# A hybrid encoder block on one core: weight sums moved between the pairs of an MLP, a value projection taken into the input stage, and an operand loaded one step earlier

## The chip, the cores and the metric

The kernel runs on one core of one Trainium2 chip. The metric is the device time of one execution in microseconds, as the median of several runs. The engines are named as in the profile: PE is TensorE's matrix multiplication and PEld its weight load, DVE is VectorE, ACT is ScalarE, POOL is GpSimd, and SP is SyncE, whose queue issues all the transfers here.

## The reference, cut to what matters

The block has 1024 tokens of width 1024. One projection of the normed input feeds two mixers: a bidirectional gated delta rule with 8 heads (mixer A), and a dilated window attention with 3 groups of 4 heads (mixer B). Then comes an MLP of width 4096.

```python
h = rmsnorm(x, ln_mix_pre)
proj = h @ w_in                      # q, k, v, z, 32 decay/beta columns (AF), mixer B's q, k, v, gates
o_a = rmsnorm(delta_rule(q, k, v, decay, beta)) * silu(z)     # both directions summed
o_b = windows combined over three groups                      # values: columns C_VB
y = (gate_a * (o_a @ w_branch_a) + gate_b * (o_b @ w_branch_b)) @ w_out
x = x + rmsnorm(y, ln_mix_post)
f = relu(rmsnorm(x, ln_mlp_pre) @ w_ff1) ** 2
x = x + rmsnorm(f @ w_ff2, ln_mlp_post)
```

All inputs and outputs are 32-bit floats.

## The kernel before

**Products.** Each operand of a large product is split into a rounded part and a remainder (`split`, L86 on ACT and L87 on DVE), and each product is three matrix instructions (`mm3`, L110 to L112): hi by hi, hi by lo, lo by hi. A projection (`proj`) loads 128 columns of weights, splits them, and takes 8 blocks of the inner dimension by 3 instructions for each half of 512 tokens, 48 instructions in all, into a PSUM bank.

**Order.** Tiles come from pools with a fixed number of buffers. When the kernel is built, a planner lays the instructions of each engine into one order, by the order of the program and by its own estimate of when operands are ready; each engine then runs its list in that order, and so does SP's queue of transfers. An instruction that waits holds back what stands behind it on its engine.

**Input stage.** `input_norm` loads 8 tiles of x, norms them, transposes them (L216) and writes the operand hT in two halves (b = 0, 1). After each half it runs the AF projection (128 columns, of which 32 are used; the result `ab` is transposed, columns on partitions) and one half of branch gate 0. `gates` transposes `ab` back (L253) and works out the decays. Twelve further gate projections stand at low priority as work for PE to fall back on (`gm`). Then `key_phase` runs for 8 heads; after every second one an attention head starts. `att_values` computes mixer B's values for two heads at a time: for each of 8 blocks of tokens, 8 by 3 instructions with hT as the weights and 256 columns of w_in moving.

**Delta stage.** For each head `delta_proj` (q, v, z), `delta_prep`, `delta_chain` (8 dependent steps) and `delta_tail`; the chain of head h runs beside the projections of head h+1. For the last head z's projection stands behind `delta_prep`. hT's memory is then given up, `oa` and `ob` tiles take its place, and `merge_b` loads and splits `ob` (four tiles) ahead of its first product; the last chain runs beside `merge_b`.

**MLP.** Both products use a scheme of seven block products for a two by two split. The sums of blocks that it needs are made on DVE. For w_ff1's product, "pair" c (`ff1_pair`, 3 to 15) loads two 512 KB tiles of w_ff1, forms s1 to s4 (L1137 to L1140, tiles `mid`), and runs seven products of 12 instructions (L1151) in the order a11, s3, s2, a22, s1, a12, s4; `keep` copies a bank on ACT before the next product adds onto it. `f_blocks` then forms the sums of the results and stores seven blocks (`d_f`). `w_blocks` makes w_ff2's sums for the second product, 16 blocks of 1 MB: load `wq`, four subtractions (L983 to L986), four stores (`d_T`). It is stepped once behind each pair, twice behind pairs 3, 4 and 5. `wq` shares one buffer (tag `t1`). `ff2` then runs the seven products over 8 pieces each, from `d_f`, w_ff2 and `d_T`; in the last product the last two pieces run bank by bank (6 times 8 and then 4 banks), so that each bank's `block` (L1043, L1045) and `finish` (L1052) can start.

Of the kernel before, what the change touches and what calls it, by code (L numbers as in the profile page):

```python
# [70 lines left out]
class Kern:  # L71
# [109 lines left out]
    def input_norm(self):  # L181
# [4 lines left out]
        self.ab = self.abp.tile([128, S], F, name="ab")  # L186
        with ExitStack() as es:
# [55 lines left out]
    def gates(self):  # L243

        nc, a, cp = self.nc, self.a, self.cp
        with ExitStack() as es:
            p = self.pool("gates", ctx=es)
            ab = self.ab
# [255 lines left out]
    def att_values(self, g, j, p):  # L504
# [6 lines left out]
        W = [self.wtile(wv[:, 4 * b:4 * b + 4, col:col + 256], [128, 4, 256]) for b in range(2)]  # L511
        V = p.tile([128, 8, 256], F, name="V", tag="V", bufs=1)
        d = self.d_v[g, j // 2]
        for b in range(4):
# [144 lines left out]
    def delta_proj(self, h, p, z_later=False):  # L659
# [12 lines left out]
        W = self.wsplit(self.wload(w_in, C_ZA + 128 * h, 8))  # L672
        z_proj = lambda: self.proj(w_in, C_ZA + 128 * h, self.hT, 8, (0, 1), z_evac, W=W)
        if not z_later:
            z_proj()
        return qT, vT, zs, z_proj
# [160 lines left out]
    def merge_b(self, p, tp, between):  # L837

        nc, a = self.nc, self.a
        PT = lambda shape, tag, bufs, dt=F: p.tile(shape, dt, name=tag, tag=tag, bufs=bufs)  # L840
        H, L = PT([128, 4, S], "ob_hi", 1, R), PT([128, 4, S], "ob_lo", 1, R)
        for k in range(4):
            cut = lambda x: [x[:, k, 0:512], x[:, k, 512:1024]]
            self.load_split(self.d_ob[k].rearrange("p (n i) -> p n i", n=2), cut(H), cut(L))
        for d in range(8):
# [6 lines left out]
            self.proj(a["w_branch_b"], 128 * d, (H, L), 4, (0, 1), evac)  # L852
# [120 lines left out]
    def w_blocks(self, p, pt):  # L973

        nc, V = self.nc, self.nc.vector
        for k in range(16):
            w = pt.tile([128, 4, 512], F, name="wq", tag="t1", bufs=1)
# [9 lines left out]
            for n, x in (("t3", t3), ("t1", b12), ("t2", b22), ("t4", b21)):  # L987
# [3 lines left out]
    def ff2(self, p, pe, tmp):  # L991
# [9 lines left out]
        def product(bank, fn, w, first, last=False):  # L1001
            def pieces(j):
                fr = p.tile([128, 2, 512], F, name="f_raw", tag="mid", bufs=3)
# [3 lines left out]
                for k in range(2):  # L1007
                    x = [p.tile([128, 512], R, name=f"f_{n}", tag=f"x_{n}", bufs=5) for n in ("hi", "lo")]
# [9 lines left out]
            n = 6 if last else 8  # L1018
            for j in range(n):
# [3 lines left out]
            if last:  # L1023
                rest = pieces(6) + pieces(7)
                for t in range(4):
                    for i, x in enumerate(rest):
                        mul(t, *x, False, i == 3)
# [64 lines left out]
    def mid_blocks(self, h, pt, p):  # L1092
# [6 lines left out]
        t1 = pt.tile([128, 4, 512], F, name="t1", tag="t1", bufs=1)  # L1099
        new = lambda: p.tile([128, 2, 512], F, name="mid", tag="mid", bufs=3)  # L1100
# [27 lines left out]
    def ff1_pair(self, c, rhs, pf, p, tmp):  # L1128
# [5 lines left out]
        sA, sB = (p.tile([128, 2, 4, 128], F, name="mid", tag="mid", bufs=3) for _ in range(2))  # L1134
# [9 lines left out]
        def product(i, bank, src, r, first):  # L1144
            pool, tag, bufs = (self.wp, "w", 2) if i in (0, 3) else (p, "x", 5)
            X = [pool.tile([128, 4, 128], R, name=f"{tag}_{n}", tag=f"{tag}_{n}", bufs=bufs) for n in ("hi", "lo")]
            self.split(*X, src)
            for k in range(4):
                for n, (x, y) in enumerate(((0, 0), (0, 1), (1, 0))):
                    start = first and k == 0 and n == 0  # L1150
                    nc.tensor.matmul(bank, X[x][:, k], r[y][:, k], start=start, stop=k == 3 and n == 2,  # L1151
                                     skip_group_check=not first)

# [5 lines left out]
        f0, f1 = (pf.tile([128, S], F, name="f", tag="f", bufs=2) for _ in range(2))  # L1159
# [4 lines left out]
        p7 = keep(B)  # L1164
        product(2, A, s2, rhs["t2"], False)
# [13 lines left out]
        self.f_blocks(c, f0[:, lo], f1[:, lo], f0[:, hi], f1[:, hi], pf)  # L1179

    def mlp(self, h, early, pf, tmp):
# [3 lines left out]
        with ExitStack() as es:  # L1185
# [21 lines left out]
            sums = self.w_blocks(p, pt)  # L1207
# [18 lines left out]
def build(tc, a, dbg=None):  # L1226
    with ExitStack() as ctx:
# [51 lines left out]
        with ExitStack() as es:  # L1279
            p = k.pool("delta", ctx=es)  # L1280
            qT, vT, zs, _ = k.delta_proj(0, p)
            state = k.delta_prep(0, p, qT, vT)
            for h in range(NH):
                out = k.delta_chain(h, p, **state)
                z = zs
                if h < NH - 1:
                    qT, vT, zs, z_proj = k.delta_proj(h + 1, p, h == NH - 2)
                    state = k.delta_prep(h + 1, p, qT, vT)
                    if h == NH - 2:
                        z_proj()  # L1290
# [3 lines left out]
                        pb = k.pool("ob", ctx=es_b, side="right")  # L1294
# [63 lines left out]
```

## Time and profile before

| | |
|---|---|
| median of 3 runs | 2233.14 us (2232.93 to 2233.23) |
| profiled execution | 2226.74 us, span 2225.0 us |
| PE, PEld | 2154.0 us (97%), 1818.4 us (82%) |
| DVE, ACT, POOL | 1504.5 us (68%), 869.3 us (39%), 61.2 us (3%) |
| matrix instructions | 11571 |
| DMA | 381.65 MB, mean 172 GB/s |
| granted clock | 0.991 of full speed |

The span is the time from the first to the last instruction of the profiled execution; its own time is 1.7 us more, and the median of the runs lies 6.4 us above that. Durations below come from the profiled execution. PE's busy time counts each instruction from its start to a modelled end, and ends overlap the next start, so an instruction's cost in a stream is read from the distance between starts.

### The profile page before, as it was taken

What the parts mean: (1) busy time and instruction counts of PE and PEld (TensorE: products, weight loads), DVE (VectorE), ACT (ScalarE), POOL (GpSimd) and SP (SyncE); (2) the same over time, 40 slices, a digit from 0 to 9 for tenths busy, and PEclk for the clock granted to TensorE, in tenths of its full rate; (3) what the DMA queues carried; (4) which work ended last, traced back from release to release, by engine and by line L of the source; (5) the groups of instructions that cost most, each with busy time, mean ns of one, the idle gap of its engine ahead of it and who ended that gap; (6) DMA issues with size and microseconds to landing.
All of it is one profiled execution on the core that took longest, in us unless ns stands there. A gap on an engine that the chain in (4) does not pass through costs nothing.

```text
span 2225.0 us, 31006 instructions
## 1 busy us (share of the span) xinstructions
PE 2154.0 (97%) x11571; PEld 1818.4 (82%) x11571; DVE 1504.5 (68%) x2656; ACT 869.3 (39%) x1820; POOL 61.2 (3%) x90
## 2 busy tenths in 40 slices
PE   7999999999999999999999999999988999999998
PEld 6877888889778878888888877989866777888877
DVE  5647563999599546777777764475966767544565
ACT  5333343322412333333333332344544555444443
POOL 0211211000000000000000000000000000000000
PEclk9999999999999999999999999999998999999999
DMA  5554746343722657434344338573667877866674
GB/s 179 175 170 129 232 128 192 125 136 100 186 81 76 168 171 196 131 104 115 114 114 119 100 114 282 168 237 105 193 213 260 275 264 260 280 193 191 194 253 139
DMA packets 339486, 381.65 MB, mean 172 GB/s; under 512 B 85540, under 2 KB 243196, under 8 KB 338312
## 3 DMA queue, kind: packets, MB, share of 16 engines
q1 hardware_dynamic: 339336, 379.67, 55.2%
q8 instruction: 91, 1.49, 0.3%
q14 instruction: 59, 0.48, 0.1%
HBM read 264.03 MB, written 118.73 MB: 172 GB/s over the span
## 4 chain that ended last, share of the span: by engine, by line
PE 77%; DVE 9%; DMA 8%; ACT 4%; issue 2%; SPq 1%; DVEq 0%; ACTq 0%
PE mm L112 13%; PE mm L110 13%; PE mm L111 13%; PE acc L1016 5%; PE mm L1016 4%; PE tr L1016 4%; PE acc L1151 3%; PE tr L808 2%; PE gm L110 2%; PE gm L112 2%; PE gm L111 2%; DMA w_raw<-in_w_ff 2%; PE ao L586 2%; DMA wq<-in_w_ff 2%; PE acc L110 1%
## 5 line engine op out<-in xcount | busy, mean ns | idle before, releaser
L110 PE MATMUL mm<-hT_hi,w_hi 128*128 128x512 f32 x960 | 391.1, 407 | 1.4 <-ACT xpad L336 1.0
L111 PE MATMUL mm<-hT_lo,w_hi 128*128 128x512 f32 x960 | 388.5, 405 | 0.0
L112 PE MATMUL mm<-hT_hi,w_lo 128*128 128x512 f32 x960 | 387.5, 404 | 0.7 <-DVE w_lo L87 0.7
L87 DVE TENSOR_TENSOR w_lo<-w_raw,w_hi 128x1024 fp32r<-128x1024 f32 (+1 forms) x219 | 253.6, 1158 | 148.3 <-ACT w_hi L86 146.4
L86 ACT CAST w_hi<-w_raw 128x1024 fp32r<-128x1024 f32 (+1 forms) x219 | 215.1, 983 | 322.5 <-PE mm L111 191.7
L110 PEld LDWEIGHTS mm<-hT_hi,w_hi 128*128 128x128 f32 x960 | 181.5, 189 | 34.6 <-ACT xpad L336 1.5
L112 PEld LDWEIGHTS mm<-hT_hi,w_lo 128*128 128x128 f32 x960 | 181.3, 189 | 34.0 <-DVE w_lo L87 2.8
L111 PEld LDWEIGHTS mm<-hT_lo,w_hi 128*128 128x128 f32 x960 | 181.6, 189 | 31.3 <-issue 0.9
L87 DVE TENSOR_TENSOR f_lo<-f_raw,f_hi 128x512 fp32r<-128x512 f32 x112 | 77.0, 692 | 115.8 <-ACT f_hi L86 115.7
L341 DVE SCALAR_TENSOR_TENSOR cu<-xpad,conv,cu 128x1024 f32<-128x1024 f32 x96 | 125.3, 1306 | 3.3
L86 ACT CAST f_hi<-f_raw 128x512 fp32r<-128x512 f32 x112 | 69.5, 621 | 148.3 <-PE tr L1016 79.4
L432 DVE TENSOR_TENSOR XA<-XB 128x62 f32<-128x62 f32 (+30 forms) x124 | 106.2, 857 | 20.2 <-ACT XB L428 17.7
L110 PE MATMUL mm<-w_hi,hT_hi 128*128 128x256 f32 x384 | 108.0, 282 | 0.3 <-ACT V L522 0.3
L435 DVE TENSOR_TENSOR XB<-XB,XA 128x62 f32<-128x62 f32 (+30 forms) x124 | 106.2, 857 | 3.0
L112 PE MATMUL mm<-w_hi,hT_lo 128*128 128x256 f32 x384 | 107.9, 281 | 0.0
L111 PE MATMUL mm<-w_lo,hT_hi 128*128 128x256 f32 x384 | 107.9, 281 | 0.0
L577 ACT ACTIVATE P<-lg,st 128x256 f32<-128x256 f32 (+1 forms) x96 | 45.4, 473 | 111.2 <-DVE st L574 109.3
L110 PE MATMUL gm<-hT_hi,w_hi 128*128 128x512 f32 x208 | 83.4, 401 | 0.7 <-ACT bg L653 0.5
L112 PE MATMUL gm<-hT_hi,w_lo 128*128 128x512 f32 x208 | 81.9, 394 | 0.0
L111 PE MATMUL gm<-hT_lo,w_hi 128*128 128x512 f32 x208 | 81.7, 393 | 0.0
L1016 PE MATMUL acc<-w_hi,f_hi 128*128 128x512 f32 x192 | 75.3, 395 | 3.1 <-ACT w_hi L86 3.1
L1016 PE MATMUL acc<-w_lo,f_hi 128*128 128x512 f32 x192 | 75.2, 392 | 0.0
(357 smaller groups left out, 5016.3 us busy)
## 6 DMA issues: line engine op xcount, KB each, us to landing
w_raw<-in_w_in SPq DMA_DIRECT2D x85, 512.0 KB
w_raw<-in_w_ff SPq DMA_DIRECT2D x62, 512.0 KB
wq<-in_w_ff SPq DMA_DIRECT2D x32, 512.0 KB
f_raw<-d_f_s SPq DMA_DIRECT2D x32, 512.0 KB
w_raw<-d_t SPq DMA_DIRECT2D x32, 512.0 KB
d_f_s<-s SPq DMA_DIRECT2D x48, 256.0 KB
d_t<-wq SPq DMA_DIRECT2D x48, 256.0 KB
f_raw<-d_f_a SPq DMA_DIRECT2D x24, 512.0 KB
```

The source lines that it names most:

```text
L86: self.nc.scalar.copy(H, src)
L87: self.nc.vector.tensor_tensor(L, src, H, op=OP.subtract)
L110: t.matmul(p, lH, rH, start=first, stop=False)
L111: t.matmul(p, lH, rL, start=False, stop=False)
L112: t.matmul(p, lL, rH, start=False, stop=last)
L341: nc.vector.scalar_tensor_tensor(u, xp[:, t:t + S], cw[:, t:t + 1], u, op0=OP.mult, op1=OP.add)
L432: nc.vector.tensor_tensor(tv, XB[:, 0:j, j:j + 1].to_broadcast([128, j, n]), XB[:, j:j + 1, j + 1:64].to_broadcast([128, j, n]), op=OP.mult)
L435: nc.vector.tensor_tensor(dst, dst, tv, op=OP.add)
L577: nc.scalar.activation(P[:, 0:W], lg[:, 0:W], AF.Exp, bias=nm, scale=-1.0, accum_out=Z)
L586: nc.tensor.matmul(o[:, oc:oc + 128], V[:, kt], PT[:, 128 * n:128 * n + 128], start=n == 0, stop=n == len(keys) - 1)
L1016: nc.tensor.matmul(bank[t], x, y, start=start and first and n == 0, stop=stop and n == 2, skip_group_check=not first)
L1151: nc.tensor.matmul(bank, X[x][:, k], r[y][:, k], start=start, stop=k == 3 and n == 2, skip_group_check=not first)
```

## The change

It has three parts. First, the input stage: the AF projection and its transposes go. Instead, 288 columns (the 256 value columns of mixer B's first two heads and the 32 AF columns) are loaded and split once, and for each of the 8 token blocks 24 instructions with hT as weights and 288 columns moving give the values, which go to memory, and the AF results, with tokens on partitions, which stay in `tok`. `att_values` for those two heads only loads them. Second, the delta stage: z's projection of the last head stands with its q and v, and `load_ob` runs before the last `delta_prep` and no longer inside `merge_b`. Third, the MLP: `w_blocks` is cut in two steps (load; sums and stores) that are called between the products of a pair, with two buffers; t3 is formed in place from t2; `f_blocks` of a pair is called after the second product of the next one. In exchange `mid` has 2 buffers where it had 3, and the split operands `x` 4 where they had 5; the last product's bank-by-bank part covers one piece where it covered two.

```diff
@@ input_norm
-                    W = self.wload(a["w_in"], C_AF, 8)
+                    wv = a["w_in"].rearrange("(k p) c -> p k c", p=128)
+                    W = p.tile([128, 8, 288], F, name="wv_raw")
+                    nc.sync.dma_start(W[:, :, 0:256], wv[:, :, C_VB:C_VB + 256])
+                    nc.sync.dma_start(W[:, :, 256:288], wv[:, :, C_AF:C_AF + 32])
...
-                if b == 0:
-                    W = self.wsplit(W)
...
-                self.proj(a["w_in"], C_AF, self.hT, 8, (b,),
-                          lambda hf, q: nc.scalar.copy(self.ab[:, 512 * hf:512 * hf + 512], q), W=W)
                 if b == 0:
                     Wg = self.wsplit(Wg, self.gp, 1)
+                    w2 = [p.tile([128, 8, 288], R, name=f"wv_{n}") for n in ("hi", "lo")]
+                    for n in range(2):
+                        self.split(*(x[:, 4 * n:4 * n + 4] for x in (*w2, W)))
                 self.branch_gate(0, W=Wg, halves=(b,))
+                for t in range(4 * b, 4 * b + 4):
+                    q = self.pp.tile([128, 288], F, name="mm", tag="mm", bufs=self.mm_bufs)
+                    tok = slice(128 * t, 128 * t + 128)
+                    for k in range(8):
+                        self.mm3(q, [x[:, k, tok] for x in self.hT], [x[:, k] for x in w2], k == 0, k == 7)
+                    v = p.tile([128, 256], F, name="v0", tag="v0", bufs=2)
+                    nc.scalar.copy(v, q[:, 0:256])
+                    nc.vector.tensor_copy(self.tok[:, t], q[:, 256:288])
+                    nc.sync.dma_start(self.d_v[0, 0][tok], v)
@@ gates
-            tok = p.tile([128, 8, 32], F, name="tok")
-            for b in range(2):
-                q = self.pp.tile([128, 512], F, name="tr", tag="sm", bufs=4)
-                for t in range(4):
-                    nc.tensor.transpose(q[:, 128 * t:128 * t + 128],
-                                        ab[:, 512 * b + 128 * t:512 * b + 128 * t + 128], self.ident)
-                nc.vector.tensor_copy(tok[:, 4 * b:4 * b + 4, :],
-                                      q.rearrange("p (t c) -> p t c", t=4)[:, :, 0:32])
+            tok = self.tok
@@ att_values
+        if g == 0 and j == 0:
+            nc.sync.dma_start(V, d.rearrange("(n p) c -> p n c", p=128))
+            return V
@@ build
-                    qT, vT, zs, z_proj = k.delta_proj(h + 1, p, h == NH - 2)
-                    state = k.delta_prep(h + 1, p, qT, vT)
+                    qT, vT, zs = k.delta_proj(h + 1, p)
                     if h == NH - 2:
-                        z_proj()
                         k.ctx_h.close()
...
+                        ob = k.load_ob(pb)
+                    state = k.delta_prep(h + 1, p, qT, vT)
@@ w_blocks
-            w = pt.tile([128, 4, 512], F, name="wq", tag="t1", bufs=1)
+            w = pt.tile([128, 4, 512], F, name="wq", tag="t1", bufs=2)
...
-            t3 = p.tile([128, 2, 512], F, name="mid", tag="mid", bufs=3)[:, 0]
-            V.tensor_tensor(t3, b22, b12, op=OP.subtract)
+            yield
             V.tensor_tensor(b12, b12, b11, op=OP.subtract)
             V.tensor_tensor(b22, b22, b12, op=OP.subtract)
+            V.tensor_tensor(b11, b22, b11, op=OP.subtract)
             V.tensor_tensor(b21, b21, b22, op=OP.subtract)
...
@@ ff2
-            n = 6 if last else 8
-            for j in range(n):
+            for j in range(7 if last else 8):
...
-                rest = pieces(6) + pieces(7)
+                rest = pieces(7)
...
@@ mlp
+            def between(i):
+                if i == 0 or i == 2 and c % 4 == 0:
+                    next(sums, None)
+                if i == 1 and due:
+                    self.f_blocks(*due)
+                if i == 4 or i == 6 and c % 4 == 0:
+                    next(sums, None)
             for c in range(3, 16):
-                self.ff1_pair(c, rhs, pf, p, tmp)
-                next(sums, None)
-                if c < 6:
-                    next(sums, None)
+                due = self.ff1_pair(c, rhs, pf, p, tmp, between)
+            self.f_blocks(*due)
```

`between(i)` is called behind product i of each pair. The tiles f0 and f1 of a pair are now taken behind its second product.

## Rows read from the trace of the kernel before

**Rows 1.** Page, part 1: busy time of each engine, share of the span

```profile
PE 2154.0 (97%) x11571; PEld 1818.4 (82%) x11571; DVE 1504.5 (68%) x2656; ACT 869.3 (39%) x1820; POOL 61.2 (3%) x90
```

**Rows 2.** Waits of PE, whole span: us in total, times, longest us

```profile
PE acc L1151 <- ACT x_hi L86: 19.7, 6, 7.5
...
PE acc L1151 <- ACT keep L1156: 6.9, 6, 1.9
...
PE acc L1016 <- ACT w_hi L86: 3.1, 1, 3.1
```

**Rows 3.** PE timeline, a run of 256 columns: start us, us, instruction

```profile
100.12 0.28 PE L112 MATMUL mm<-w_hi,hT_lo 128*128 128x256 f32 x1
...
105.56 0.28 PE L112 MATMUL mm<-w_hi,hT_lo 128*128 128x256 f32 x1
```

**Rows 4.** PE timeline, a run of 512 columns

```profile
2200.22 0.39 PE L1016 MATMUL tr<-w_lo,f_hi 128*128 128x512 f32 x1
...
2206.12 0.39 PE L1016 MATMUL mm<-w_hi,f_hi 128*128 128x512 f32 x1
```

**Rows 5.** Window of all pairs, line L1151 alone

```profile
1622.67:1907.54 284.87, 258.20 (x1092) 207.53 (x1091) 0.96 0.78 263
```

**Rows 6.** PE timeline in pair 4; brackets: idle before and its releaser

```profile
1652.18 0.80 PE L1151 MATMUL acc<-t_hi,x_hi 128*128 128x512 f32 x1 [7.53 <-ACT x_hi L86]
```

**Rows 7.** DVE timeline between pairs 3 and 4

```profile
1650.18 0.69 DVE L983 TENSOR_TENSOR mid<-wq 128x512 f32<-128x512 f32 x1 [4.16 <-DMA wq<-in_w_ff]
1650.79 0.69 DVE L1137 TENSOR_TENSOR mid<-w_raw 128x512 f32<-128x512 f32 x1
```

**Rows 8.** Waits of SP's queue, 1622 to 1730 us

```profile
SPq L988 <- DVE mid L983: 30.5, 7, 7.2
```

**Rows 9.** Windows in the pairs

```profile
1652.00:1660.00 8.00, 6.63 (x18) 4.49 (x19) 6.70 (x12) 3.21 (x7) 0.00 (x0) 0.60 0.72 220
1727.00:1765.00 38.00, 38.00 (x169) 31.49 (x168) 25.54 (x42) 19.84 (x36) 0.00 (x0) 1.00 0.85 290
1765.00:1908.00 143.00, 136.06 (x593) 110.42 (x592) 100.52 (x158) 79.82 (x140) 0.00 (x0) 1.00 0.79 267
```

**Rows 10.** ACT timeline in pair 9

```profile
1771.25 0.62 ACT L86 CAST w_hi<-w_raw 128x512 fp32r<-128x512 f32 x1 [1.30 <-DMA w_raw<-in_w_ff]
1771.77 1.06 ACT L1156 COPY keep<-acc 128x512 f32<-128x512 f32 x2
```

**Rows 11.** Instructions of L253: ns min/median/max, first and last start us

```profile
L253 PE MATMUL tr<-cst,ab x8: 270/273/273, 45.2 to 45.9; 128*128 128x128 f32 x8
```

**Rows 12.** Windows: length, busy us (instructions), PEclk, DMA share, GB/s

```profile
0.00:15.00 15.00, 4.46 (x16) 2.86 (x16) 6.56 (x16) 9.49 (x18) 0.34 (x6) 1.00 0.91 316
15.00:30.00 15.00, 14.88 (x64) 12.33 (x65) 11.01 (x24) 11.93 (x23) 0.00 (x0) 1.00 0.74 212
```

**Rows 13.** Page, part 3: DMA packets, MB, share of 16 engines

```profile
q1 hardware_dynamic: 339336, 379.67, 55.2%
```

**Rows 14.** Window of the last head's chain

```profile
1292.00:1305.50 13.50, 9.20 (x52) 6.72 (x50) 12.06 (x32) 6.02 (x14) 0.00 (x0) 1.00 0.44 144
```

**Rows 15.** Instructions that touch ob_hi

```profile
L87 DVE TENSOR_TENSOR ob_lo<-w_raw,ob_hi x8: 683/684/693, 1294.0 to 1303.3; 128x512 fp32r<-128x512 f32 x8
```

**Rows 16.** DVE timeline in pair 8

```profile
1748.81 0.69 DVE L966 TENSOR_TENSOR s<-f 128x512 f32<-128x512 f32 x1 [0.16 <-ACT f L959]
...
1757.34 0.69 DVE L1168 TENSOR_TENSOR f<-keep,acc 128x512 f32<-128x512 f32 x1 [1.95 <-PE acc L1151]
```

**Rows 17.** Timeline of the last microseconds

```profile
2216.34 0.68 DVE L1045 TENSOR_TENSOR fy<-tr,ln_mlp_post 128x512 f32<-128x512 f32 x1
...
2216.98 0.39 PE L1016 MATMUL tr<-w_hi,f_lo 128*128 128x512 f32 x1
...
2219.07 0.68 DVE L1045 TENSOR_TENSOR fy<-tr,ln_mlp_post 128x512 f32<-128x512 f32 x1
```

**Rows 18.** ACT timeline in the second product's seventh part

```profile
2149.03 1.04 ACT L86 CAST w_hi<-w_raw 128x1024 fp32r<-128x1024 f32 x1 [9.65 <-DMA w_raw<-in_w_ff]
```

More of the change, by code (lines that the diff above doesn't have):

```diff
@@ L510, in att_values @@
         col = C_VB + 128 * (4 * g + j)
-        W = [self.wtile(wv[:, 4 * b:4 * b + 4, col:col + 256], [128, 4, 256]) for b in range(2)]
         V = p.tile([128, 8, 256], F, name="V", tag="V", bufs=1)
         d = self.d_v[g, j // 2]
+        if g == 0 and j == 0:
+            nc.sync.dma_start(V, d.rearrange("(n p) c -> p n c", p=128))
+            return V
+        W = [self.wtile(wv[:, 4 * b:4 * b + 4, col:col + 256], [128, 4, 256]) for b in range(2)]
         for b in range(4):
@@ L671, in z_evac @@
             nc.vector.scalar_tensor_tensor(zs[:, s], zs[:, s], 1.0, q, op0=OP.add, op1=OP.mult)
-        W = self.wsplit(self.wload(w_in, C_ZA + 128 * h, 8))
-        z_proj = lambda: self.proj(w_in, C_ZA + 128 * h, self.hT, 8, (0, 1), z_evac, W=W)
-        if not z_later:
-            z_proj()
-        return qT, vT, zs, z_proj
+        self.proj(w_in, C_ZA + 128 * h, self.hT, 8, (0, 1), z_evac)
+        return qT, vT, zs
     def delta_prep(self, h, p, qT, vT):
@@ L835, in load_split, with load_ob @@
             self.split(H[n], L[n], t[:, n])
-    def merge_b(self, p, tp, between):
-        nc, a = self.nc, self.a
+    def load_ob(self, p):
         PT = lambda shape, tag, bufs, dt=F: p.tile(shape, dt, name=tag, tag=tag, bufs=bufs)
@@ L844, in merge_b @@
             self.load_split(self.d_ob[k].rearrange("p (n i) -> p n i", n=2), cut(H), cut(L))
+        return H, L
+    def merge_b(self, ob, tp, between):
+        nc, a = self.nc, self.a
         for d in range(8):
@@ L981, in w_blocks @@
             b11, b12, b21, b22 = (w[:, n] for n in range(4))
[L982 to L983 removed]
+            yield
             V.tensor_tensor(b12, b12, b11, op=OP.subtract)
             V.tensor_tensor(b22, b22, b12, op=OP.subtract)
+            V.tensor_tensor(b11, b22, b11, op=OP.subtract)
             V.tensor_tensor(b21, b21, b22, op=OP.subtract)
[L987 removed]
+            for n, x in (("t1", b12), ("t2", b22), ("t3", b11), ("t4", b21)):
                 nc.sync.dma_start(self.d_T[n][k], x)
@@ L1002, in pieces @@
             def pieces(j):
-                fr = p.tile([128, 2, 512], F, name="f_raw", tag="mid", bufs=3)
+                fr = p.tile([128, 2, 512], F, name="f_raw", tag="mid", bufs=2)
                 nc.sync.dma_start(fr, self.d_f[fn][2 * j:2 * j + 2].rearrange("k p i -> p k i"))
@@ L1007, in pieces @@
                 for k in range(2):
-                    x = [p.tile([128, 512], R, name=f"f_{n}", tag=f"x_{n}", bufs=5) for n in ("hi", "lo")]
+                    x = [p.tile([128, 512], R, name=f"f_{n}", tag=f"x_{n}", bufs=4) for n in ("hi", "lo")]
                     self.split(*x, fr[:, k])
@@ L1098, in mid_blocks @@
         T = [[pt.tile([128, 4, 512], R, name=f"t{n}_{x}") for x in ("hi", "lo")] for n in (2, 3, 4)]
-        t1 = pt.tile([128, 4, 512], F, name="t1", tag="t1", bufs=1)
-        new = lambda: p.tile([128, 2, 512], F, name="mid", tag="mid", bufs=3)
+        t1 = pt.tile([128, 4, 512], F, name="t1", tag="t1", bufs=2)
+        new = lambda: p.tile([128, 2, 512], F, name="mid", tag="mid", bufs=2)
         add = lambda o, x, y: nc.vector.tensor_tensor(o, x, y, op=OP.add)
@@ L1126, in mid_blocks, with ff1_pair @@
             yield
-    def ff1_pair(self, c, rhs, pf, p, tmp):
+    def ff1_pair(self, c, rhs, pf, p, tmp, between):
         nc = self.nc
@@ L1133, in ff1_pair @@
         a11, a12, a21, a22 = (x[:, s] for x in w for s in (slice(0, 4), slice(4, 8)))
-        sA, sB = (p.tile([128, 2, 4, 128], F, name="mid", tag="mid", bufs=3) for _ in range(2))
+        sA, sB = (p.tile([128, 2, 4, 128], F, name="mid", tag="mid", bufs=2) for _ in range(2))
         s3, s1, s2, s4 = sA[:, 0], sA[:, 1], sB[:, 0], sB[:, 1]
@@ L1152, in product @@
                                      skip_group_check=not first)
+            between(i)
         def keep(bank):
@@ L1157, in keep @@
             return t
-        f0, f1 = (pf.tile([128, S], F, name="f", tag="f", bufs=2) for _ in range(2))
         lo, hi = slice(0, 512), slice(512, 1024)
@@ L1164, in ff1_pair @@
         p7 = keep(B)
+        f0, f1 = (pf.tile([128, S], F, name="f", tag="f", bufs=2) for _ in range(2))
         product(2, A, s2, rhs["t2"], False)
@@ L1178, in ff1_pair @@
         self.relu2(f0[:, hi], A)
-        self.f_blocks(c, f0[:, lo], f1[:, lo], f0[:, hi], f1[:, hi], pf)
+        return c, f0[:, lo], f1[:, lo], f0[:, hi], f1[:, hi], pf
     def mlp(self, h, early, pf, tmp):
@@ L1206, in mlp @@
                        b21=[x[:, 4:8] for x in h[0]], b22=[x[:, 4:8] for x in h[1]])
-            sums = self.w_blocks(p, pt)
+            sums = self.w_blocks(pt)
+            due = None
+            def between(i):
[5 more added lines that the diff above has]
+                    next(sums, None)
             for c in range(3, 16):
-                self.ff1_pair(c, rhs, pf, p, tmp)
-                next(sums, None)
-                if c < 6:
-                    next(sums, None)
+                due = self.ff1_pair(c, rhs, pf, p, tmp, between)
+            self.f_blocks(*due)
             for _ in sums:
@@ L1304, in between @@
                             k.delta_tail(h, p, *out, z, oa)
-                    k.merge_b(pb, p, between)
+                    k.merge_b(ob, p, between)
             k.dump("oa", k.d_oa)
```

16 lines of the change are left out of this document (7 added, 9 removed).

## The prediction

> **What bounds the kernel now.** I read the page first: PE is busy for 97% of the span, DVE for 68%, ACT for 39% [rows 1]. So time is won in two ways only: fewer PE instructions, or less of the time in which PE stands. Next come PE's waits, sorted by size. The largest by far belongs to one line, the MLP's pairs (L1151): 19.7 us in six waits for a split operand `x_hi`, and 6.9 us in six waits for a bank's copy `keep`; the second product (L1016) has one of 3.1 us [rows 2]. Then the timeline gives the cost of an instruction in a stream. From the first to the last of 49 instructions with 256 columns pass 5.44 us, 113 ns each [rows 3]; over 27 with 512 columns 5.90 us, 227 ns each [rows 4]. The durations shown in those rows (280 and 390 ns) overlap and are no price.
>
> With that the pairs are weighed as one stage: 1092 instructions in 284.87 us [rows 5]. At 227 ns they need 247.9, so 37.0 us are there to be won: the 26.6 of the two waits, and 10.4 around them. One place shows both. In pair 4 PE stands 7.53 us for `x_hi` [rows 6]. On DVE the sums of w_ff2 (L983) had waited 4.16 us for their load `wq`, and directly behind them stood L1137, which forms s3, whose split PE wanted [rows 7]. SP's queue shows the other end: its stores of the sums waited 30.5 us in seven times for L983 [rows 8]; `wq` has one buffer, so the next load waits for those stores. Behind such a wait the granted clock was 0.60, between the levels of 1.2 and 2.4 GHz, and 18 instructions took most of 8 us [rows 9]: that is the 10.4. Where the order fits, nothing of this is left: from 1727 to 1765 PE is busy throughout at full clock, with the transfers at 290 GB/s and a DMA share of 0.85 [rows 9]. The `keep` waits have another cause: ACT stood 1.30 us for the load of a later pair's weights, and the two copies behind it came late [rows 10].
>
> **Input stage.** The AF projection goes: 48 instructions at 227 ns, 10.9 us. Its 8 transposes start within 0.7 us [rows 11], so 0.8 with the last. The values' 192 instructions move ahead and grow from 256 to 288 columns. No row has 288; the bounds are 113 ns and 227 ns [rows 3, 4], and on the line between them it is 128, which I take, since 288 is next to 256: 24.6 us for 21.7, 2.9 more. With the ends it would be 0 or 21.9 more. PE: -10.9 - 0.8 + 2.9 = -8.8.
>
> What this moves on other engines: three splits of 1024 elements a row become two of 1152 and 1152, eight small copies on each of ACT and DVE stand for six and two, and SP's queue issues eight stores of 128 KB and one load of 1 MB more for the values, two 512 KB loads of weights less later. All lie beside PE's 30 us of new and old matrix work, with ACT busy 11.9 of 15 us in the tightest stretch [rows 12]. The load grows by 0.66 MB, 2.1 us at the 316 GB/s of the first 15 us [rows 12], and by 1024 packets; all packets took 55.2% of 16 engines' span [rows 13], 58 ns each, so 3.7 us by that count. The second half of x stands behind it and lands 2 to 4 us later; PE's cover then is the gate's first half and four blocks of values, 24 x 0.227 + 96 x 0.128 = 17.7 us. Without cover it would cost up to 4. The decays start later by the moved work; nothing on PE's early path needs them. I take -9, with -12 and 0 as ends.
>
> **Delta stage.** In the 13.5 us of the last chain PE is busy for 9.2, so 4.3 us stand open, while DVE is busy for 12.06 [rows 14], 5.5 of it the eight splits of `ob` (684 ns each, from 1294.0 on) [rows 15]. They start there because `ob` takes hT's place and z's projection reads hT last. With z 10.9 us of matrix work earlier, `ob` can be split before the chain, and `merge_b`'s products can fill it. Against it: z covered `delta_prep`, whose operands come from DVE, and the splits now stand in DVE's and ACT's queues in front of that preparation. From -4.3 to +5, half of z's 10.9 us of cover; I take -3, as the splits leave a DVE that was full.
>
> **The pairs.** The work is the same: four subtractions a block, equal loads and stores, 4 + 7 + 3 + 4 DVE instructions and the block's four in a pair. What moves is order. (1) A block's two loads stand behind product 0 and its sums and four stores behind product 4, so 48 instructions, 10.9 us, lie between (24, 5.4 us, in pairs 4, 8 and 12, which take two blocks); the load is 1.05 MB, 3.6 us alone at 290 GB/s, and with the second buffer it may start once the block before the last is stored. So the sums' wait falls away, and L1137 is no longer behind it. (2) `f_blocks` moves past the next pair's weight loads, its four sums and its first two splits: seven stores fewer ahead of the weights in SP's queue. Its inputs come only when the former pair's last product is done, so it ran this late before as well (L966 in pair 8 starts 0.16 us after ACT delivers) [rows 16]; it now waits with less behind it. (3) Two `mid` and four `x` buffers: a split still runs four operand products ahead. I leave 9 us of the 37.0 standing: the `keep` waits are about weights that arrive late, which the change does not touch (6.9), and the three double pairs move 7.08 MB each, which at 290 / 0.85 = 341 GB/s needs 20.8 us against 19.1 of PE; part of that 5 us is smoothed by the buffers. So -28; the ends are -36 and -22, the latter with a wait of `keep`'s 1.15 us in each of 13 pairs.
>
> **Second product and end.** `f_raw` is now two deep. In steady state the weights are two deep as well, so nothing changes; at the one wait there, ACT stood 9.65 us for weights behind the rows' loads and stores [rows 18], and a piece less of f ahead can add between 0 and 24 x 0.227 = 5.4 us. I take 0.5, as the weights came first. At the end DVE handles a bank in 2.73 us, 2216.34 to 2219.07, as fast as PE delivered them (12 x 0.227 = 2.72), and the last starts 1.9 us after PE's end at 2217.2 [rows 17]. Now PE delivers every 1.36 us: the first bank is done 4.1 us before the end, DVE starts some 0.7 later, and the fourth starts 3 x 2.73 = 8.2 after that, 4.8 behind PE's end. That is 2.9 later, nothing covers it, and 2.0 if DVE's short waits for ACT are filled; I take 2.5.
>
> **Sum.** -9 - 3 - 28 + 0.5 + 2.5 = -37. The profiled execution's own time, 2226.7, becomes 2189.7; the median of the runs lies 6.4 above it, so 2233.1 becomes **2196**. Its own range is 2187 to 2206.
>
> **Rivals.**
> - *The double pairs wait as pairs 4 to 6 did.* Those lost 19.7 + 10.4 = 30 us, 10 each. If the load of the second block is late, L1168 and the splits behind the sums wait, and the pairs win between 0 and 18 us: 2206 to 2224, 2215 in the middle. For: 7.08 MB in 19.1 us are 371 GB/s, above the 316 and 290 of [rows 9, 12]. Against: DMA share was 0.79 and below while PE waited. The Trainium skill (DMA: Bandwidth & Descriptors, Specifications) puts a core's HBM limit at about 358 GB/s; by that a double pair takes 19.8 us, 0.7 more than PE, and the 290 GB/s here neither reaches nor refutes it. Chance 0.18.
> - *The values were the filler.* Around 100 us [rows 3] the 21.7 us of values ran among the key phases. If neither the next projections nor the low-priority gates take that place, and 9 us stand open, the input stage gives nothing: 2205; at 14 us it is 2210. Against: 12 gate projections of 10.9 us are free for it. Chance 0.09.
> - *Everything fits.* Pairs -36, chain -4, start -11, end +2: 2184. For: the 38 us in which PE never waits. Chance 0.09.
> - *Slower: the seven stores.* f0 and f1 are written again by L1168, behind product 3, once the former pair's stores are out. From L966 to L1168 are 8.5 us [rows 16]; four sums (2.4) and 1.84 MB at 290 GB/s (6.3) fill them. If SP issues the stores late, DVE's queue stands, with the splits behind. A split in hand covers one product, 2.7 us; beyond it every microsecond counts 13 times. It is slower overall once a pair loses 3.9 us, so with stores 6.6 us late; at 5 us a pair it is 13 x 24.1 - 285 = +28, and with the rest 2252. Against: no store held L1168 in pair 8, PE did. Chance 0.07.
> - *The gains cancel*, the change only moving waits: 2233. Chance 0.02.
>
> **How the numbers follow.** The forecast has 0.55. The range takes it whole, the filler's case, half of the double pairs' and half of the best: 2184 to 2215, 0.77 to 0.8. A measurement of this kernel tells 0.2%, 4.5 us, from no change. Faster: 0.55 + 0.17 + 0.09 + 0.09 = 0.90, taken as 0.89; within: 0.03; slower: 0.08.
>
> **What would show it.** The stretch of L1151 falls to some 257 us, with `x_hi` gone from PE's waits and `keep` still there; no L253, and a matrix group of 288 columns at 128 ns; PE's open time in the last chain under 2 us; the last bank's L1045 nearly 5 us behind PE's end. It is wrong if L983 or L1168 waits for a transfer in many pairs, or if PE stands between 60 and 110 us.

## The result, and the profile after

The median went from 2233.18 us (2232.93 to 2234.99, 4 runs) to **2201.93 us** (2199.93 to 2202.59, 4 runs): ratio 0.9857, 95% interval [0.984, 0.9874], faster by 31.3 us where 37 were forecast.

The two profiled executions differ by less, 2226.74 and 2202.59 us (spans 2225.0 and 2200.4): the one of before was 6.4 us quicker than its median, the one of after 0.7 slower. Three landmarks on PE cut the span of each into four stretches: the starts of the first instruction of the pairs, of the one behind their last, and of PE's last.

| stretch | before | after | difference | forecast |
|---|---|---|---|---|
| up to the pairs | 1622.7 | 1615.7 | -7.0 | -12 |
| the pairs | 284.9 | 260.6 | -24.3 | -28 |
| second product | 309.4 | 314.2 | +4.8 | +0.5 |
| end | 8.0 | 10.0 | +2.0 | +2.5 |

The page's first part, for [rows 1]: PE lost 56 instructions and 12 us, the AF projection's 48 and the 8 transposes.

```profile
PE 2142.0 (97%) x11515; PEld 1812.0 (82%) x11515; DVE 1507.5 (69%) x2661; ACT 869.3 (40%) x1823; POOL 58.5 (3%) x90
```

Waits of PE over the whole span, for [rows 2], and the window of the pairs, L1156 alone, for [rows 5].

```profile
PE acc L1156 <- ACT keep L1162: 8.7, 8, 3.5
...
PE acc L1022 <- ACT f_hi L86: 6.8, 1, 6.8
```

```profile
1615.67:1876.27 260.60, 251.86 (x1092) 205.21 (x1091) 0.99 0.80 273
```

No row for `x_hi` is left, and the clock in the pairs rose from 0.96 to 0.99. `keep` stayed. And a wait stands that before did not have: 6.8 us for `f_hi` in the second product.

Of what is left in the pairs, 12.7 us, the largest part sits in one of them. Pair 6 took 24.43 us, 5.4 over the 19.07 of 84 instructions at 227 ns; pairs 11 and 3 follow with 3.1 and 1.8. The timeline of pair 6, across four engines:

```profile
1682.33 0.46 SPq L977 DMA_DIRECT2D d_f_s<-f  x1
1682.88 0.38 SPq L94 DMA_DIRECT2D w_raw<-in_w_ff  x1
...
1690.20 0.69 DVE L1142 TENSOR_TENSOR mid<-w_raw 128x512 f32<-128x512 f32 x1 [5.72 <-DMA w_raw<-in_w_ff]
...
1690.93 0.62 ACT L86 CAST x_hi<-mid 128x512 fp32r<-128x512 f32 x1 [6.76 <-DVE mid L1142]
...
1695.19 0.50 PE L1156 MATMUL acc<-h_hi,x_hi 128*128 128x512 f32 x1 [3.49 <-ACT keep L1162]
```

Read it downwards: the next pair's weights were issued behind the stores of `f_blocks`, landed 7 us later, held DVE's s3, which held ACT's split, and a `keep` behind that held PE. This is one execution: in the other kernels with the MLP part, pair 6 lost 0.9 to 3.1 us. Windows of pair 7 and of two stretches round the last chain (columns as in [rows 12]), and the splits of `ob`, for [rows 14, 15]:

```profile
1285.00:1298.60 13.60, 10.13 (x48) 8.21 (x45) 8.02 (x17) 7.58 (x27) 0.00 (x0) 0.75 0.46 143
...
1292.00:1305.50 13.50, 13.50 (x71) 11.64 (x71) 9.46 (x26) 3.35 (x7) 0.00 (x0) 0.82 0.40 121
...
1699.65:1718.70 19.05, 19.05 (x85) 15.77 (x84) 14.90 (x25) 9.64 (x17) 0.00 (x0) 1.00 0.95 335
```

```profile
L87 DVE TENSOR_TENSOR ob_lo<-w_raw,ob_hi x8: 684/685/693, 1279.2 to 1289.0; 128x512 fp32r<-128x512 f32 x8
```

The chain's stretch is full where it was 9.20 of 13.5, and `ob` is split before it. The open time moved ahead, into the last `delta_prep`: 3.5 us of 13.6. Behind it the granted clock was lower: 0.82 in the filled stretch, where it was 1.00 before [rows 14]. The new matrix group of 288 columns, 32 instructions from the first row to the last, 31 steps of 132 ns (forecast 128):

```profile
47.84 0.30 PE L112 MATMUL mm<-wv_hi,hT_lo 128*128 128x288 f32 x1
...
51.94 0.29 PE L110 MATMUL mm<-wv_hi,hT_hi 128*128 128x288 f32 x1
```

### The profile page after: what moved, and what is told of

It is laid out like the page before. It is cut to its first block, busy times and chain, and to the rows that moved or that the text cites. A ratio compares the mean times of both kernels' runs of the same rounds, so it can differ in the third digit from the quotient of the medians.

```text
span 2200.4 us, 30966 instructions
## 1 busy us (share of the span) xinstructions
PE 2142.0 (97%) x11515; PEld 1812.0 (82%) x11515; DVE 1507.5 (69%) x2661; ACT 869.3 (40%) x1823; POOL 58.5 (3%) x90
## 4 chain that ended last, share of the span: by engine, by line
PE 82%; DVE 7%; DMA 5%; ACT 4%; issue 2%; SPq 1%; DVEq 0%; ACTq 0%
PE mm L112 13%; PE mm L110 13%; PE mm L111 13%; PE acc L1156 6%; PE acc L1022 5%; PE mm L1022 4%; PE tr L1022 4%; PE tr L811 2%; PE gm L110 2%; PE gm L112 2%; PE gm L111 2%; PE ao L592 2%; PE acc L110 1%; PE ch L790 1%; PE acc L111 1%
## 5 line engine op out<-in xcount | busy, mean ns | idle before, releaser
L110 PE MATMUL mm<-hT_hi,w_hi 128*128 128x512 f32 x944 | 383.3, 406 | 2.5 <-DVE rk L179 1.3
L111 PE MATMUL mm<-hT_lo,w_hi 128*128 128x512 f32 x944 | 381.8, 404 | 0.0
L112 PE MATMUL mm<-hT_hi,w_lo 128*128 128x512 f32 x944 | 381.6, 405 | 0.1
L87 DVE TENSOR_TENSOR w_lo<-w_raw,w_hi 128x1024 fp32r<-128x1024 f32 (+1 forms) x216 | 245.8, 1138 | 115.7 <-ACT w_hi L86 114.4
L110 PE MATMUL mm<-w_hi,hT_hi 128*128 128x256 f32 x320 | 91.2, 286 | 1.6 <-ACT V L528 1.6
L111 PE MATMUL mm<-w_lo,hT_hi 128*128 128x256 f32 x320 | 90.6, 283 | 0.0
L112 PE MATMUL mm<-w_hi,hT_lo 128*128 128x256 f32 x320 | 90.5, 283 | 0.0
```

Source lines behind the costliest of these rows:

```text
L87: self.nc.vector.tensor_tensor(L, src, H, op=OP.subtract)
L110: t.matmul(p, lH, rH, start=first, stop=False)
L111: t.matmul(p, lH, rL, start=False, stop=False)
L112: t.matmul(p, lL, rH, start=False, stop=last)
```

## The experiments

Stretches as in the table above. Each group of runs has runs of the kernel before on the same chip beside it; the ratios are to those, their medians 2228.2 to 2230.9.

| run | median us (lowest to highest) | ratio to before | pairs | second product | end |
|---|---|---|---|---|---|
| before_again | 2229.67, one run | | 287.9 | 307.2 | 8.0 |
| a_only | 2226.35 (2215.46 to 2230.07) | 0.9979 [0.9967, 0.9991] | 287.3 | 308.4 | 8.0 |
| d_only | 2223.87 (2220.11 to 2227.47) | 0.9977 [0.9965, 0.9989] | 286.6 | 308.4 | 8.0 |
| c_only | 2202.71 (2199.08 to 2205.90) | 0.9877 [0.9863, 0.9892] | 252.9 | 313.6 | 9.9 |
| c_d | 2199.86 (2195.13 to 2200.90) | 0.9859 [0.9841, 0.9877] | 252.8 | 313.1 | 9.9 |
| one_buffer | 2203.18 (2201.34 to 2205.17) | 0.9879 [0.9862, 0.9895] | 258.2 | 313.3 | 9.9 |
| old_places | 2197.41 (2193.84 to 2198.72) | 0.9850 [0.9833, 0.9867] | 255.8 | 312.6 | 10.0 |
| f_back | 2196.74 (2194.38 to 2197.90) | 0.9847 [0.9829, 0.9866] | 257.2 | 314.1 | 10.0 |
| t3_only | 2200.01 (2198.76 to 2203.72) | 0.9872 [0.9847, 0.9896] | 259.4 | 308.8 | 8.0 |
| t3_d | 2196.31 (2194.81 to 2201.84) | 0.9859 [0.9843, 0.9875] | 259.7 | 309.7 | 8.0 |
| deep_f | 2195.25 (2193.01 to 2196.19) | 0.9844 [0.9824, 0.9863] | 256.2 | 309.7 | 9.9 |
| mended | 2193.35 (2190.45 to 2195.87) | 0.9837 [0.9823, 0.9850] | 256.2 | 311.4 | 8.4 |

**The parts alone.** First the kernel before, unchanged:

> The kernel before, unchanged, for a second profile. Its first profile spans 2225.0 us, while its timed runs lie 6 to 8 us above that. Theory 1: the extra time lies in the pairs (284.9 us in the first profile), whose waits for transfers differ from run to run; then a span near 2231 shows some 290 us there and the other stages within 1 us. Theory 2: it is spread over the stages or lies ahead of the pairs, and the pairs stay within 1 us of 284.9.

Its span is 2.9 us longer than in the profile shown above: 2.1 ahead of the pairs, 3.0 in them, -2.2 in the second product. Neither theory fits. That is the spread to which a stretch of one profile can be read. The input part alone:

```diff
-                    W = self.wload(a["w_in"], C_AF, 8)
+                    W = p.tile([128, 8, 288], F, name="wv_raw")
...
-                self.proj(a["w_in"], C_AF, self.hT, 8, (b,), ...
+                    for k in range(8):
+                        self.mm3(q, [x[:, k, tok] for x in self.hT], [x[:, k] for x in w2], k == 0, k == 7)
```

> The kernel before with the input stage's part alone (288 columns at the start, no AF projection, no transposes of its result). Theory 1, instruction count: -8.8 us by the forecast; 2224 us, ratio 0.996. Theory 2, from the profile after (start of the pairs 7.0 us earlier for the input and delta parts together, end of the key phases 10.6 earlier, start of the delta stage 6.0 earlier): about -6, with some 3 us of the gain given back in waits between the key phases and the inverse. Rival: the values were a filler that nothing replaces; then 0.

By the ratio it is 0.21% faster, 4.7 us, half of the term of 9. PE's last transpose of the keys comes 4.7 us earlier in its profile, but the delta stage starts 0.6 later than in the first profile of before; the two profiles of before differ there by 2.1. All fourteen profiles together tell more: the delta stage starts at 859.9 us on the mean of the seven kernels with the input part (857.0 to 863.6) and at 863.1 on that of the seven without it (861.2 to 865.4), so 3.2 us earlier, while the keys end 5 to 11 us earlier than in the first profile of before. Part of what the input stage wins is given back in between. Its waits of PE, with the keys' longest wait at 5.4 where before it was 3.4 (6.5 in all in both):

```profile
PE acc L1157 <- ACT x_hi L86: 19.7, 6, 6.1
...
PE tr L352 <- DVE kT L346: 6.5, 3, 5.4
```

The delta part alone:

```diff
-        if not z_later:
-            z_proj()
+        self.proj(w_in, C_ZA + 128 * h, self.hT, 8, (0, 1), z_evac)
...
+                        ob = k.load_ob(pb)
+                    state = k.delta_prep(h + 1, p, qT, vT)
```

> The kernel before with the delta stage's part alone (z ahead of the last preparation, ob loaded earlier). Theory 1, the forecast: -3 us, ratio 0.9987, as the products of merge_b fill the last chain. Theory 2, from the profile after: the waits only move, from the chain to the preparation ahead of it, where PE now stands some 5 us for ACT; then -1 or nothing.

By the ratio it is 0.23% faster, 5.1 us; the pairs start at 1618.4, 4.3 earlier. The MLP part alone, with no other hunk, and then with the delta part:

```diff
-            w = pt.tile([128, 4, 512], F, name="wq", tag="t1", bufs=1)
+            w = pt.tile([128, 4, 512], F, name="wq", tag="t1", bufs=2)
...
+            yield
...
+            V.tensor_tensor(b11, b22, b11, op=OP.subtract)
```

> The kernel before with the MLP's part alone (two buffers, sums and f_blocks between products, shorter last part, two-deep f). Theory 1: pairs from 284.9 to about 260 us, the second product 5 us longer for its later f, the end 2 us longer: -17.5 by the profiles, and up to -24 if the timed runs of before are longer in the pairs than its profile. Rival: the pairs' gain rests on the earlier parts (another phase of the transfers); then the pairs stay above 270.

> The kernel before with the MLP's and the delta stage's parts, without the input stage's. The changed kernel measured 0.9857 of before, the MLP's part alone 0.9877, the delta part alone 0.9977, the input part alone 0.9979. If the parts add, this is 0.9854 and the input part then adds nothing beside them; if the delta part's gain is a shift that the others undo, it is near 0.9877.

The MLP part carries nearly all, and its pairs take 252.9 us where theory 1 had 260. With the delta part beside it the time is that of the full change (0.9859 and 0.9857): next to the others the input part adds nothing that these ratios can tell. Their intervals reach 0.0017 to either side, 4 us, so the 3.2 us of the profiles are not excluded.

**Which edit of the MLP part.** From the changed kernel, one edit is undone at a time.

```diff
-            w = pt.tile([128, 4, 512], F, name="wq", tag="t1", bufs=2)
+            w = pt.tile([128, 4, 512], F, name="wq", tag="t1", bufs=1)
```

> The changed kernel with the second buffer of wq taken away (places of the sums and of f_blocks as changed). Theory 1, the second buffer is what frees the pairs: loads wait for stores again, L989 waits for its load, and the pairs lose 15 us or more against the 253 to 261 us of the changed kernel. Theory 2, the places are what count, as the sums no longer stand ahead of the next pair's s3: the pairs stay within 8 us.

```diff
-                due = self.ff1_pair(c, rhs, pf, p, tmp, between)
-            self.f_blocks(*due)
+                self.f_blocks(*self.ff1_pair(c, rhs, pf, p, tmp, lambda i: None))
+                for _ in range(4 if c < 6 else 2):
+                    next(sums, None)
```

> The changed kernel with the sums and f_blocks called behind each pair as before (twice behind pairs 3 to 5), the second buffer kept. Theory 1 (buffer): the loads come early enough, the 8 to 14 us losses of three pairs shrink to a few us each, and the pairs take 265 or less. Theory 2 (places): the two blocks behind pairs 3 to 5 still hold L1142 up, and the pairs stay above 275.

```diff
-                due = self.ff1_pair(c, rhs, pf, p, tmp, between)
-            self.f_blocks(*due)
+                self.f_blocks(*self.ff1_pair(c, rhs, pf, p, tmp, between))
```

> The changed kernel with f_blocks alone put back behind its pair; the sums' places and the second buffer stay. Theory 1: its place is worth little, since its inputs are late anyway (within 4 us of 253 to 261). Theory 2: it then stands ahead of the next pair's s3 and splits, and each pair loses about 1 us or more, 13 in all.

My theory of the two causes, places and second buffer, lost here: with either undone the pairs stay at 255.8 to 258.2 us, and the old places are not slower than the new ones. Two explanations were left: each of the two suffices by itself, or neither matters and a third edit, common to all these kernels, does it. The third edit is t3, which before took one of the three `mid` buffers and now is made in place. It was tried alone, on the kernel before, with one `wq` buffer, the old places and the old depths:

```diff
-            t3 = p.tile([128, 2, 512], F, name="mid", tag="mid", bufs=3)[:, 0]
-            V.tensor_tensor(t3, b22, b12, op=OP.subtract)
             V.tensor_tensor(b12, b12, b11, op=OP.subtract)
             V.tensor_tensor(b22, b22, b12, op=OP.subtract)
+            V.tensor_tensor(b11, b22, b11, op=OP.subtract)
```

> The kernel before with one edit: t3 of the weights' sums is made in place, over b11 (after t1 and t2), and takes no buffer of the tag `mid`; one buffer for the sums' weights, one call behind each pair, the x tiles five deep, all as before. Theory A (either the second buffer or the places suffices, since each undone alone left the pairs at 256 to 258 us): with neither of them the pairs stay at 280 to 288 us in the profile and the time at 2226 to 2233, ratio 0.998 to 1.001. Theory B (the pairs waited because t3 took the third `mid` buffer, so that the next pair's s3, s1, s2, s4 had to wait for t3's store): the pairs fall to 253 to 265 us, the waits of PE for x_hi go from 19.7 us to 5 or less, and the time is 2203 to 2213, ratio 0.987 to 0.992.

Theory B's forecast came true: these few lines alone give the ratio of the whole MLP part (0.9872 and 0.9877). Its waits of PE in the pairs, for [rows 2], and their window, for [rows 5]:

```profile
PE acc L1150 <- ACT keep L1155: 6.6, 9, 1.2
...
PE mm L1150 <- ACT x_hi L86: 1.5, 1, 1.5
```

```profile
1620.90:1880.30 259.40, 251.24 (x1092) 203.82 (x1091) 1.00 0.86 290
```

How it acts is seen in DVE's order. In the kernel before, L1137 starts 0.61 us behind the second block's L983 in pair 4 [rows 7], and in the two pairs after it:

```profile
1677.63 0.69 DVE L983 TENSOR_TENSOR mid<-wq 128x512 f32<-128x512 f32 x1 [1.06 <-DMA wq<-in_w_ff]
1678.24 0.68 DVE L1137 TENSOR_TENSOR mid<-w_raw 128x512 f32<-128x512 f32 x1
...
1705.03 0.69 DVE L983 TENSOR_TENSOR mid<-wq 128x512 f32<-128x512 f32 x1 [1.11 <-DMA wq<-in_w_ff]
1705.64 0.68 DVE L1137 TENSOR_TENSOR mid<-w_raw 128x512 f32<-128x512 f32 x1
```

The wait that theory B gives as the reason, for t3's store, is not what pair 4 shows. L1137 started at 1650.79; the store of the second block's t3 was issued after it, and that of the first block's 14.8 us ahead of it. The last split of pair 3 that reads a `mid` tile had ended 20 us earlier:

```profile
1629.60 0.69 DVE L87 TENSOR_TENSOR x_lo<-mid,x_hi 128x512 fp32r<-128x512 f32 x1
...
1650.90 0.32 SPq L988 DMA_DIRECT2D d_t<-mid  x1
```

So L1137 was late by its place in DVE's list, behind an L983 that waited for its load. In t3_only the next pair's s3 (here L1136) stands ahead of this pair's last results (L1174), of `f_blocks` (L966) and of the second block (L982, L983). The sums still wait for their load, but nothing of the pair is behind them:

```profile
1639.00 0.68 DVE L1136 TENSOR_TENSOR mid<-w_raw 128x512 f32<-128x512 f32 x1
...
1640.81 0.68 DVE L1174 TENSOR_TENSOR f<-keep,mm 128x512 f32<-128x512 f32 x1
...
1644.91 0.69 DVE L966 TENSOR_TENSOR s<-f 128x512 f32<-128x512 f32 x1
...
1647.97 0.69 DVE L982 TENSOR_TENSOR wq<-wq 128x512 f32<-128x512 f32 x1
...
1651.46 0.69 DVE L983 TENSOR_TENSOR wq<-wq 128x512 f32<-128x512 f32 x1 [1.60 <-DMA wq<-in_w_ff]
```

The time from the start of s3 to the start of the product that needs it, per pair, and the pair's time above 19.07 us:

| | pair 4 | 5 | 6 | 7 | 8 |
|---|---|---|---|---|---|
| before: lead, loss | 1.4, 11.6 | 1.4, 8.3 | 1.4, 8.3 | 8.6, 0 | 8.8, 0 |
| t3_only: lead, loss | 4.9, 0 | 4.6, 2.9 | 3.5, 1.6 | 4.9, 1.9 | 7.2, 0 |
| one_buffer: lead, loss | 4.9, 0 | 5.7, 1.8 | 1.8, 2.9 | 9.1, 0 | 8.7, 1.7 |
| after: lead, loss | 7.8, 0.6 | 14.7, 0 | 13.9, 5.4 | 12.2, 0 | 14.5, 0.8 |

A lead of 1.4 us is hardly more than s3 (0.69) and its split on ACT (0.62) take: PE was standing for it, and the pair lost 8 to 12 us. Longer ones were worth little more: after leads by 8 to 15 us in these pairs and loses as much as t3_only. The lead alone does not set the loss: one_buffer led by 1.8 us in pair 6 and lost 2.9. Why t3's buffer sets the order is read from the code, not tried by itself: a tag's buffers are handed out in the order of the program, and s3's was next behind the second block's t3, so the planner could not list it ahead. The edit also makes t3 the third subtraction where it was the first, and no run gives t3 a buffer of its own and leaves the rest, so the two are not told apart by a run. Behind pairs 3 to 5, two t3 and the pair's two tiles draw four times on three buffers; the losses are in pairs 4 to 6. The Trainium skill (Perfetto Trace Analysis, Optimization Strategy) says that a gap repeating for a stretch can mean that there is no room to allocate the next tile. The trace agrees in part: three pairs in a row lost 8 to 12 us, and it went when t3 left the tag, with three buffers as before; but when L1137 ran no buffer was being waited for, and what held it was its place in the list.

**The second product and the end.** From the changed kernel, three `f_raw` for all products but the first:

```diff
-                fr = p.tile([128, 2, 512], F, name="f_raw", tag="mid", bufs=2)
+                fr = (p if fn == "a11" else pe).tile([128, 2, 512], F, name="f_raw",
+                     tag="mid" if fn == "a11" else "fr", bufs=2 if fn == "a11" else 3)
```

> The changed kernel with f_raw of the second product three deep, from the pool opened at its start, for all partial products but the first (which is loaded ahead, in the pairs). If the second product's wait of 6.8 us for f_hi comes of f_raw's two buffers, it falls to 3 us or less, the second product from 314 to 308 to 311 us, and the time to 2195 to 2199 (ratio to before 0.983 to 0.985). If it comes of the loads' place on SP's queue, behind the stores of the first half's results, which wait for their values, the wait stays at 6 to 7 us and the time within 2 us of the changed kernel's 2202.

In the kernel after, the wait runs through SP's queue, here with ACT and PE behind it:

```profile
2099.68 3.75 SPq L1058 DMA_DIRECT2D out<-fy  x6
...
2107.23 1.44 SPq L1067 DMA_DIRECT2D fx<-d_x  x3
2108.76 0.90 SPq L1010 DMA_DIRECT2D f_raw<-d_f_a  x2
...
2116.54 1.14 ACT L86 CAST f_hi<-f_raw 128x512 fp32r<-128x512 f32 x2 [10.54 <-DMA f_raw<-d_f_a]
...
2117.21 0.80 PE L1022 MATMUL acc<-w_hi,f_hi 128*128 128x512 f32 x1 [6.80 <-ACT f_hi L86]
```

With a third buffer the loads still stand behind those stores, but a piece more is at hand, so the first expectation holds for the wait and the stretch. The ratio alone (0.9844) can't be told from the full change's. `f_hi` is gone from PE's waits, and what is left is the wait for the weights that before had too (3.1) [rows 2]:

```profile
PE acc L1022 <- ACT w_hi L86: 3.0, 1, 3.0
```

Last, two kernels that put this together. The first is t3_only with the delta part (its hunks as in d_only). The second is the changed kernel with `f_blocks` back (as in f_back), `f_raw` three deep (as in deep_f) and the last pieces as before:

```diff
-            for j in range(7 if last else 8):
+            for j in range(6 if last else 8):
...
-                rest = pieces(7)
+                rest = pieces(6) + pieces(7)
...
-                        mul(t, *x, False, i == 1)
+                        mul(t, *x, False, i == 3)
```

> The kernel before with t3 in place and the delta part of the change; places, one buffer, depths, last pieces and input stage as before. If t3's place is the whole gain of the pairs and the delta part adds its own 4 to 5 us, the pairs stay at 255 to 260 us, the second product at 307 to 310, the tail at 8, and the time is 2193 to 2198 (ratio 0.983 to 0.986), below the full change's 2202. If the second buffer, the places and the input part carry something beside t3, it stays above the full change's time.

> The changed kernel with three edits: f_blocks behind its own pair again, f_raw of the second product three deep, the last product's last two pieces bank by bank again (6 and 2, as before). If the wait for f_hi and the last bank's way out are the terms that I sized wrongly and as I sized them, the second product is 308 to 311 us, the tail falls from 10.0 to 8.0, and the time is 2190 to 2194 (ratio 0.981 to 0.983). If the last bank by itself is not on the path, the tail stays at 10 and the time at 2194 to 2197.

t3_d, which keeps the places, the single buffer and the input stage of before, can't be told from the full change: 0.9859 and 0.9857. The profile of t3_d is that of its slowest run. mended is the fastest kernel here, though its interval overlaps deep_f's. Its end is 8.4 us for 9.9, but its second product 311.4 for 309.7; the sums are 319.8 and 319.6. So the last pieces' place is not shown to be worth anything.

## Why the prediction came out as it did

**The pairs: the size right, the cause wrong.** Of the 37.0 us, 24.3 were won by the first profiles and 32.0 in c_only, so -28 met what was measured. The claim that L1137 would no longer stand behind the sums' wait was right too. That the sums' wait falls away was not: in the kernel after, the sums (L989, L990) still waited for their load eight times, in five pairs, 9.0 us in all, where L983 had waited ten times, 25.9 us. That is nearly the prediction's own sign of being wrong; it did little harm because s3 no longer stood behind it. The step that failed is (1): it put the gain on the places and the second buffer. Either undone left it whole, and t3 in place, which the prediction counted as nothing ("the work is the same: four subtractions a block"), brings it alone. No run has the places and the second buffer with t3 left in `mid`, so whether they could have won the pairs without it stays open. I had read the row of L983 and L1137 [rows 7] as a queue, and did not ask why the planner had put them in that order; a clue stands in that same row, the tile's name `mid`. What the other MLP edits add in the pairs, 259.4 to between 252.8 and 260.6, they give back in the second product and at the end.

**The second product: mis-sized.** +0.5 became +4.8 between the first profiles (the stretch is 312.6 to 314.2 us in all kernels with two `f_raw`), inside the stated 0 to 5.4. The sentence that failed is "in steady state the weights are two deep as well, so nothing changes"; the cost came at the one place that is not steady, which the prediction had named and had then taken at the lower end. With three buffers deep_f took 4.5 of it back, and mended 2.8.

**The end.** +2.0 for +2.5, but not as told: the last bank's product with the norm's weights was to start nearly 5 us behind PE's end, and started 1.4 behind the start of PE's last instruction:

```profile
2190.46 0.39 PE L1022 MATMUL tr<-w_hi,f_lo 128*128 128x512 f32 x1
...
2191.83 0.68 DVE L1050 TENSOR_TENSOR fy<-tr,ln_mlp_post 128x512 f32<-128x512 f32 x1
...
2195.89 1.42 DVE L1057 SCALAR_TENSOR_TENSOR fy<-fy,r,fx 128x512 f32<-128x512 f32 x2
```

DVE ran the last L1050 ahead of three banks' closing L1057; the prediction had each bank closed before the next began. So the size came out by another order than the one it was worked out from, which is luck.

**The input stage: too large.** The matrix work fell as costed (132 ns for 128), but of 9 us 4.7 were measured alone, the ratios can't tell it from nothing beside the other parts, and the starts of the delta stage put it at 3.2. In the kernel after, the keys end 10.6 us earlier and the delta stage starts 6.0 earlier. The step that failed is that the 8.8 us less of matrix work would reach the end of the stage whole; the rival that the values had been the filler, at 0.09, is nearer than the forecast. PE's open time ahead of the delta stage took 2.4 us back (27.3 us on the mean of the seven profiles with the input part, 24.9 on that of the others). Where the rest went is not settled: all the waits that PE shows from 60 to 863 us come to 12.5 us before and 13.7 after.

**The delta stage.** -3 for 5.1 measured alone, with an interval of 2.5 to 7.8 us. Both halves of the argument hold: the chain filled, and the preparation, having lost z as cover, opened by 3.5 us. But they nearly cancel: from 1260 to 1330 us PE stood 4.3 us before, 3.1 in d_only and 3.8 after. From the first instruction of the delta stage to the first of the pairs 759.7 us pass in both profiles of before, 756.6 in d_only and 758.6 after. So the filled chain explains about 1 us of the gain; where the rest of it lies is not shown.

**The rivals.** The double pairs did not wait: pairs 4, 8 and 12 lost 0.6, 0.8 and 0.0 us. Pair 7 ran without a wait at 335 GB/s with a DMA share of 0.95. The 290 GB/s that the prediction went by was no bound in the kernel before either. Its pair 8, the end of its pairs and the start of its span moved more:

```profile
1746.20:1765.24 19.04, 19.04 (x85) 15.78 (x84) 11.92 (x20) 9.17 (x16) 0.00 (x0) 1.00 0.93 311
...
1905.00:1915.00 10.00, 10.00 (x45) 8.27 (x45) 6.40 (x10) 5.97 (x10) 0.00 (x0) 1.00 1.03 399
2.80:21.80 19.00, 11.14 (x44) 8.41 (x44) 11.90 (x23) 13.74 (x26) 0.00 (x0) 1.00 1.08 364
```

Packets are counted where they start, so a short window can show a share a little over 1. The Trainium skill (DMA: Bandwidth & Descriptors, Specifications) has the limit of a core at about 358 GB/s. The trace of before does not agree, with 399 over 10 us and 364 over 19 us; what was measured decides. The shortage of 1.7 us that the prediction gave each double pair rests on 341 GB/s and was not seen. The slower case, stores in front of what a pair needs, did occur, in pair 6 and through SP's queue, not through L1168: 5.4 us once, not 13 times.

**The sum.** The gain ahead of the pairs was counted too high and the loss behind them too low, so both errors go the same way. Between the two profiled executions the change is -24.2 us for -37. By the medians it is -31.3, because the runs of before lay 6.4 us above its profile and those of after did not. The prediction had carried the 6.4 over to the kernel after; that it came within 6 us of the median is in part luck.

## What to carry to other kernels

When an instruction stands behind an unrelated one that waits, ask first why it was listed there. Count, for each tag of buffers, how often a loop body draws on it and how many buffers it has: a tile borrowed for a side job can fix the order of the main one, and giving that tile another home was here worth nearly the whole change. And cost a buffer taken away at the worst place of the stage that uses it, not at its steady state.

## What the runs showed of the hardware that was not expected

One kernel, before, ran from 2223.82 to 2234.99 us over its runs on several chips, 0.5%; single stretches of two profiles of it differ by 2 to 3 us. So terms of 2 to 3 us can't be read from one profile each, and some that the prediction set down singly remain open for that reason. The transfers sustained 335 GB/s over a whole pair while PE ran without a wait, where the pairs of before had 311 in pair 8, also without a wait of PE, and the 10 us from 1905, round their end, 399.
